# A decoder layer on one core: order of weight splits and gate sums where the norm phase meets the up-projection

## The chip, the core and the metric

The kernel runs on one core of a Trainium2 chip. Five engines work side by side, each with its own queue in fixed order: PE multiplies matrices (its weight loads show as PEld), DVE, ACT and POOL do elementwise work, SP issues loads. They wait for each other by semaphores. The metric is the time of one execution on the device in microseconds (us), lower is better.

## What is computed

One layer: an RMS norm and a projection into three branches (a recurrent one, stick-breaking attention, attention to memory tokens), a gated merge, and a feed-forward part with a causal convolution. The change lies in the feed-forward part:

```python
def conv_ffn(x, g, w_up, conv_w, conv_b, w_down):
    h = rms_norm(x, g) @ w_up            # 1024 x 1024 by 1024 x 5632
    t = h.shape[1]
    hp = jnp.pad(h, ((0, 0), (CONV_W - 1, 0), (0, 0)))
    acc = conv_b + hp[:, 0:t] * conv_w[0]
    for i in range(1, CONV_W):
        acc = acc + hp[:, i:i + t] * conv_w[i]
    gate, val = jnp.split(acc, 2, axis=-1)
    return (jax.nn.silu(gate) * val) @ w_down
```

## The kernel before

Every fp32 product is made of three matmuls: each operand is split into a rounded high part (made by ACT, a copy into fp32r) and the rest (POOL or DVE, a subtraction), and high x high, high x low and low x high are added up in PSUM.

The up-projection (`up_phase`) works through 22 pairs of 128-row blocks of the weight, gate pairs (even n) and value pairs (odd n) in turn. A pair takes seven products instead of eight (Strassen's way in Winograd's form), each of 4 x 3 = 12 matmuls of 128x512. Product (n, i) below is step i of pair n; step 4 is written 40 (the matmuls) and 41 (what follows them). Per pair the weights are two loaded tiles w1 and w2 (named `wr` for odd, `rw` for even n), from which come sums and differences:

- `prep1(n)` splits w1: high and low part `wh`, `wl`, for products 1 and 2;
- `prep2(n)` makes two sums on POOL (L1484, L1485, tile `it`) and splits them (`l`), for products 5 and 6;
- `prep3(n)` makes w1 - w2 in place (L1497) and s4 (L1498, tile `s`), and splits the first (`wh`, `wl`, products 7 and 4) and s4 (`l`, 512 wide, product 3).

All splits go through `hl`: its activation is L1462, its subtraction on POOL L1465. `keep` holds the activation at its place in the written order, `queue` the subtraction; without them a scheduler places the instruction.

What PE makes is taken up by DVE: L1585 adds product 6 and product 1's copy `p` into `u`, L1592 and L1593 make the second block's `u` from product 7, `p` and 5's bank, L1602 takes product 4 off, L1609 adds product 3's bank. PSUM banks are used again at once: product 7 accumulates on the bank of 6, so it waits for L1585; product 3 on the bank of 5, so it waits for L1593. Then `conv_half` makes the convolution: an activation (L1529), two steps on DVE (L1530, L1531), and for a gate pair a sigmoid (L1534) and a product (L1535), for a value pair a product (L1540) into `gall`. `act_sums` makes four sums of these results behind each value pair, on DVE (L1548), and stores seven tiles to `actd` from ACT's queue. The first two sums (`late` false) stood in step 3 of the pair, the other two in step 6 of the next, behind L1585.

The stretch in question is the seam: the norm phase's last operands, pair 0 and pairs 1 and 2 are written out by hand. On PE the order there is (0,7), (0,4), (0,3), (1,6), (1,5), (1,4), (1,7), (2,1), (1,3), (2,5), (2,6), (2,2), (2,7), (2,4), (2,3), (3,1). In the code `prep3(1)` stood behind step (0,3), and `prep1(2)` behind step (1,5).

Of the kernel before, what the change touches and what calls it, by code (L numbers as in the profile page):

```python
# [49 lines left out]
class Trunk:  # L50
# [1386 lines left out]
    def up_phase(self, raws, t2, operand, split_hi, split_lo, sums, norm, spread):  # L1437
# [11 lines left out]
        pairs = [(o + 2 * f, f, o > 0) for f in range(NF // 2) for o in (0, NF)]  # L1449
        W, st = {}, {}  # L1450
# [9 lines left out]
        def hl(src, pool, tags, n=1024, keep=False, queue=False):  # L1460
            hi, lo = (pool.tile([128, n], F32R, name=self.nm(t), tag=t, bufs=16 if t == "l4" else 2) for t in tags)
            ins = nc.scalar.activation(hi, src, AF.Copy)  # L1462
            if keep:
                self.pinned(ins)
            ins = nc.gpsimd.tensor_tensor(lo, src, hi.bitcast(F32), ALU.subtract)  # L1465
            if queue:
                self.tc.keep_in_program_order(ins)
            return hi, lo
# [1 line left out]
        L, R = slice(0, 512), slice(512, 1024)  # L1470

        def prep1(n):
            w = self.early[4 * n] if n < 2 else hl(W[n][0], self.pool_wt, ("wh", "wl"), queue=n == 2)
            st[n, 1], st[n, 2] = [[x[:, c] for x in w] for c in (L, R)]

        def prep2(n):
# [12 lines left out]
        def prep3(n):  # L1489
            if n == 0:  # L1490
                w2, s4 = self.early[2], self.early[3][:, R]
            else:
                w1, w2 = W.pop(n)
                s = st.pop((n, "s"))
                s4 = self.pool_r.tile([128, 512], F32, name=self.nm("s4"), tag="s4", bufs=1)
                fix = self.tc.keep_in_program_order if n == 1 else lambda ins: ins
                fix(nc.gpsimd.tensor_tensor(w2[:, L], w1[:, L], w2[:, L], ALU.subtract))  # L1497
                fix(nc.gpsimd.tensor_tensor(s4, w1[:, R], s[:, R], ALU.subtract))  # L1498
            w = hl(w2, self.pool_wt, ("wh", "wl"), queue=n == 1)
            st[n, 7], st[n, 4] = [[x[:, c] for x in w] for c in (L, R)]  # L1500
            if n:
                st[n, 3] = hl(s4, self.pool_l, ("l4", "l4"), 512)

# [9 lines left out]
        def bank():  # L1513
            return self.ps("mm")
# [31 lines left out]
        def act_sums(f, late):  # L1546
            a11, a21, a12, a22 = (g_all[:, j] for j in range(4))
            tt = lambda o, x, y, op: self.pinned(nc.vector.tensor_tensor(o, x, y, op))  # L1548
            if not late:
                tt(sa[:, 0], a21, a22, ALU.add)  # L1550
                tt(sa[:, 1], sa[:, 0], a11, ALU.subtract)
                for j, src in ((0, a11), (1, a12), (3, a22)):
                    nc.scalar.dma_start(self.actd[f, j], src)
            else:
                tt(sa[:, 2], a11, a21, ALU.subtract)
                tt(sa[:, 3], a12, sa[:, 1], ALU.subtract)
                nc.scalar.dma_start(self.actd[f, 2], sa[:, 3])
                nc.scalar.dma_start(self.actd[f, 4:7].rearrange("i p t -> p i t"), sa[:, 0:3])
# [7 lines left out]
        def step(n, i):  # L1566
            if i == 1:
                A = st[n, "A"] = bank()
                product(n, 1, A, True, True)
                if n:  # L1570
                    evacuate(n)
            elif i == 2:
                A = st.pop((n, "A"))
                product(n, 2, A, False, True)
                u = st[n, "u1"] = u_tile(n < 2)
                nc.scalar.activation(u[:, L2], A, AF.Copy)
            elif i == 5:
                C = st[n, "C"] = bank()
                product(n, 5, C, True, True)
            elif i == 6:  # L1580
                Bk = st[n, "B"] = bank()
                product(n, 6, Bk, True, True)
                if (n, "u1") not in st:
                    st[n, "u1"] = u_tile()
                self.pinned(nc.vector.tensor_tensor(st[n, "u1"][:, R2], Bk, st[n, "p1"], ALU.add))  # L1585
                if n and pairs[n - 1][2]:
                    act_sums(pairs[n - 1][1], True)
            elif i == 7:
                Bk = st.pop((n, "B"))
                product(n, 7, Bk, False, True)  # L1590
                v = st[n, "u2"] = u_tile()
                nc.vector.tensor_tensor(v[:, L2], Bk, st.pop((n, "p1")), ALU.add)  # L1592
                nc.vector.tensor_tensor(v[:, R2], st[n, "C"], v[:, L2], ALU.add)  # L1593
            elif i == 40:
                Dk = st[n, "D"] = bank()
                product(n, 4, Dk, True, True)
            elif i in (4, 41):
                if i == 4:
                    step(n, 40)
                Dk = st.pop((n, "D"))  # L1600
                v = st[n, "u2"]
                nc.vector.tensor_tensor(v[:, L2], v[:, L2], Dk, ALU.subtract)  # L1602
                if n + 1 < len(pairs):
                    conv(n, 1, st.pop((n, "u2")))
            elif i == 3:
                C = st.pop((n, "C"))
                product(n, 3, C, False, True)
                u = st.pop((n, "u1"))
                nc.vector.tensor_tensor(u[:, R2], C, u[:, R2], ALU.add)  # L1609
                if n + 1 == len(pairs):  # L1610
                    conv(n, 1, st.pop((n, "u2")))
                st[n, "gates"] = conv(n, 0, u)
                if pairs[n][2]:
                    act_sums(pairs[n][1], False)
                    if n + 1 == len(pairs):
                        act_sums(pairs[n][1], True)

# [56 lines left out]
        nc.vector.tensor_tensor(v[:, R2], st[0, "C"], v[:, L2], ALU.add)  # L1674
        step(0, 40)
        step(0, 41)
        load(2)
        step(0, 3)
        prep3(1)
        for n in range(1, len(pairs)):  # L1680
            order = {1: (6, 5, 40, 7, 41, 3), 2: (5, 6, 2, 7, 4, 3)}.get(n, (1, 5, 6, 2, 7, 4, 3))
            nxt = n + 1
            more = nxt < len(pairs)
            for i in order:
                if i == 2:
                    u1_first(n)
                else:
                    step(n, i)
                if not more:
                    continue  # L1690
                if i == 5:
                    load(nxt + 1)
                if (n, i) == (1, 5):
                    for close in st.pop((0, "gates")):
                        close()
                elif (n, i) == (1, 41):
                    step(nxt, 1)
                if i == (6 if n > 1 else 7):
                    prep2(nxt)
                if i == (2 if n > 1 else 5):  # L1700
                    prep1(nxt)
                if i == 3:
                    prep3(nxt)
# [332 lines left out]
```

## Time and profile before

| | |
|---|---|
| time, median of 3 runs | 1805.65 us (1805.49 to 1806.79) |
| the profiled execution | 1808.55 us |
| its span, first to last instruction | 1806.8 us |
| granted clock of PE, mean | 0.996 |
| DMA, mean | 145 GB/s |

PE's waits beside those of the seam are short. In the list of who waited for whom, a row has the waiting engine and line, what it waited for, and the total, the count and the longest in us:

```profile
PE mm L115 <- POOL wl L81: 2.3, 1, 2.3
PE g L115 <- ACT at L920: 2.2, 3, 1.0
PE mm L115 <- DVE at L1286: 1.6, 3, 0.6
```

How the other rows are read: a row of the timeline has the start and the length in us, the engine, the line, the operation, out<-in and the count of instructions merged into it; in brackets the idle time before it and what ended that. A row of a window has its bounds and length, the busy time of PE, PEld, DVE, ACT and POOL (with counts), the granted clock, the DMA share and GB/s. Names lose their numbers there, so `wh<-wr` is the high part of any odd pair's tile.

### The profile page before, as it was taken

To read this page: it belongs to the slowest core of one execution; us is meant where nothing else is said; L and a number is where in the kernel's file an instruction comes from. 1 tells how busy PE (TensorE), PEld (TensorE's weight loads), DVE (VectorE), ACT (ScalarE), POOL (GpSimd) and SP (SyncE) were. 2 spreads that over 40 slices of the span, in tenths; PEclk is the share of its full clock that TensorE was granted. 3 is DMA by queue.
4 is the path that set the end of the run, shared out by engine and by line. 5 is a ranking of instruction groups with operands and counts; after the bars stand their busy time and mean duration, and the time that the engine had idled before them with its cause. 6 is when DMAs were issued, how large, how long until landed. Compare 5 with 4: busy or idle time off the path is not lost.

```text
span 1806.8 us, 27325 instructions
## 1 busy us (share of the span) xinstructions
PE 1783.4 (99%) x10479; PEld 1446.0 (80%) x10479; DVE 1182.9 (65%) x1626; ACT 864.3 (48%) x1556; POOL 791.7 (44%) x448
## 2 busy tenths in 40 slices
PE   9999999999999999999999999989999999999999
PEld 7777778888888888777777878867888888888887
DVE  5667775898987534244443872577776777795596
ACT  6444344566566535534444334543544444454343
POOL 3223353322231462122333542486767767545454
PEclk9999999999999999999999999999999999999999
DMA  5255664211112352577654553222332323486476
GB/s 208 59 163 176 196 208 157 73 42 45 53 56 88 115 129 79 192 239 277 206 187 176 186 198 106 105 87 88 123 100 88 116 101 111 134 304 226 146 237 206
DMA packets 122772, 261.29 MB, mean 145 GB/s; under 512 B 28681, under 2 KB 43657, under 8 KB 122514
## 3 DMA queue, kind: packets, MB, share of 16 engines
q1 hardware_dynamic: 85026, 193.83, 32.7%
q10 hardware_dynamic: 33840, 53.10, 8.0%
q0 software_dynamic: 3776, 12.62, 2.3%
q8 instruction: 82, 1.34, 0.3%
q14 instruction: 48, 0.39, 0.1%
HBM read 178.99 MB, written 80.48 MB: 144 GB/s over the span
## 4 chain that ended last, share of the span: by engine, by line
PE 69%; DVE 7%; ACT 3%; issue 2%; POOL 2%; DMA 1%; SPq 0%; DVEq 0%; POOLq 0%; ACTq 0%
PE mm L115 57%; PE g L115 10%; PE g L105 2%; DVE at L926 1%; DVE it L545 1%; DMA wr<-in_w_out_dram 1%; DVE mg L1294 1%; POOL wl L81 1%; DVE inst L547 1%; DMA A<-yd 0%; ACT at L1143 0%; DVE w L821 0%; DVE at L1286 0%; DVE g L1530 0%; DVE at L1287 0%
## 5 line engine op out<-in xcount | busy, mean ns | idle before, releaser
L81 POOL TENSOR_TENSOR wl<-wr,wh 128x1024 fp32r<-128x1024 f32 (+2 forms) x78 | 195.9, 2512 | 501.5 <-ACT wh L80 492.0
L115 PE MATMUL mm<-xhi,wh 128*128 128x512 f32 x784 | 260.1, 413 | 0.5 <-DVE w L322 0.4
L115 PE MATMUL mm<-xlo,wh 128*128 128x512 f32 x784 | 243.5, 392 | 0.0
L115 PE MATMUL mm<-xhi,wl 128*128 128x512 f32 x784 | 242.5, 391 | 0.0
L115 PEld LDWEIGHTS mm<-xlo,wh 128*128 128x128 f32 x784 | 147.1, 188 | 33.2 <-DVE xlo L199 0.3
L115 PEld LDWEIGHTS mm<-xhi,wl 128*128 128x128 f32 x784 | 147.0, 188 | 33.0 <-POOL wl L81 0.7
L115 PEld LDWEIGHTS mm<-xhi,wh 128*128 128x128 f32 x784 | 136.7, 190 | 29.2 <-issue 6.1
L80 ACT ACTIVATE wh<-wr 128x1024 fp32r<-128x1024 f32 (+2 forms) x78 | 81.8, 1048 | 146.4 <-PE mm L115 93.3
L115 PE MATMUL mm<-dw,da 128*128 128x512 f32 x528 | 121.0, 390 | 0.0
L115 PE MATMUL mm<-BT,wh 128*128 128x512 f32 x352 | 111.8, 399 | 6.7 <-DVE u L1585 5.8
L115 PE MATMUL mm<-BT,l 128*128 128x512 f32 x504 | 117.6, 389 | 0.0
L115 PEld LDWEIGHTS mm<-dw,da 128*128 128x128 f32 x528 | 98.9, 188 | 21.5 <-DVE da L1746 1.0
L1747 POOL TENSOR_TENSOR dw<-draw,dw 128x512 fp32r<-128x512 f32 x55 | 81.9, 1497 | 77.3 <-ACT dw L1745 75.9
L926 DVE TENSOR_TENSOR_SCAN at<-at,nrt 128x128 f32<-128x128 f32 (+3 forms) x64 | 94.2, 1479 | 25.5 <-ACT at L920 25.3
L115 PEld LDWEIGHTS mm<-BT,l 128*128 128x128 f32 x504 | 94.6, 188 | 19.7
L115 PE MATMUL mm<-B,wh 128*128 128x512 f32 x352 | 108.6, 390 | 0.0
L1746 DVE TENSOR_TENSOR da<-draw,da 128x512 fp32r<-128x512 f32 x77 | 65.9, 862 | 53.2 <-ACT da L1744 52.9
L1465 POOL TENSOR_TENSOR l<-it,l 128x1024 fp32r<-128x1024 f32 x21 | 51.2, 2436 | 92.9 <-ACT l L1462 92.8
L115 PE MATMUL g<-dw,da 128*128 128x512 f32 x396 | 90.2, 389 | 0.0
L821 DVE TENSOR_TENSOR w<-w,nrt 128x1024 f32<-128x1024 f32 x24 | 49.9, 2078 | 58.1 <-ACT w L820 47.1
L115 PEld LDWEIGHTS g<-dw,da 128*128 128x128 f32 x396 | 74.3, 188 | 15.4
L1744 ACT ACTIVATE da<-draw 128x512 fp32r<-128x512 f32 x77 | 48.1, 627 | 80.4 <-PE mm L115 32.3
(335 smaller groups left out, 3990.9 us busy)
## 6 DMA issues: line engine op xcount, KB each, us to landing
wr<-in_w_in_dram SPq DMA_DIRECT2D x48, 512.0 KB, 3.6
draw<-actd SPq DMA_DIRECT2D x77, 256.0 KB, 3.3
draw<-in_w_down_dram SPq DMA_DIRECT2D x55, 256.0 KB, 4.5
at<-scr SPq DMA_DIRECT2D x24, 512.0 KB, 5.8
wr<-in_w_up_dram SPq DMA_DIRECT2D x22, 512.0 KB, 3.5
actd<-gall ACTq DMA_DIRECT2D x44, 256.0 KB, 3.3
rw<-in_w_up_dram SPq DMA_DIRECT2D x20, 512.0 KB, 3.7
gsd<-w ACTq DMA_DIRECT2D x18, 512.0 KB, 2.8
```

Source lines behind the costliest of these rows:

```text
L80: self.nc.scalar.activation(hi, raw, AF.Copy)
L81: self.nc.gpsimd.tensor_tensor(lo, raw, hi.bitcast(F32), ALU.subtract)
L105: self.pinned(self.nc.tensor.transpose(out, in_, self.ident[:n, :n]))
L115: self.pinned(self.nc.tensor.matmul(*a, **k))
L545: self.pinned(nc.vector.tensor_tensor(tv, X[:, 0:s, s : s + 1].to_broadcast([128, s, n]), X[:, s : s + 1, s + 1 : 64].to_broadcast([128, s ...
L547: self.pinned(nc.vector.tensor_tensor(X[:, 0:s, s + 1 : 64], X[:, 0:s, s + 1 : 64], tv, ALU.add))
L821: nc.vector.tensor_tensor(g, g, self.nrb, ALU.mult)
L926: self.pinned(nc.vector.tensor_tensor_scan(sn[:, :W][:, ::-1], sn[:, :W][:, ::-1], self.nrt[:, 1152 - W :][:, ::-1], 1.0, ALU.mult, ALU.max))
L1465: ins = nc.gpsimd.tensor_tensor(lo, src, hi.bitcast(F32), ALU.subtract)
L1744: self.pinned(nc.scalar.activation(A[:, 0], a, AF.Copy))
L1746: self.pinned(nc.vector.tensor_tensor(A[:, 1], a, A[:, 0].bitcast(F32), ALU.subtract))
L1747: nc.gpsimd.tensor_tensor(Wt[:, 1], w, Wt[:, 0].bitcast(F32), ALU.subtract)
```

## The change

`prep3(1)` now makes its two differences and splits w1 - w2 ahead of step (0,3), and hands s4 back; s4's split and `prep1(2)` follow behind step (0,3). The activations of the three are held in the written order. The first two sums of the first value pair (n = 1) leave its step 3 and stand behind L1585 in step 6 of pair 2, ahead of the other two. Nothing is computed that wasn't before, and the same number of instructions runs.

```diff
         def prep1(n):
-            w = self.early[4 * n] if n < 2 else hl(W[n][0], self.pool_wt, ("wh", "wl"), queue=n == 2)
+            w = self.early[4 * n] if n < 2 else hl(W[n][0], self.pool_wt, ("wh", "wl"), keep=n == 2, queue=n == 2)
...
-            w = hl(w2, self.pool_wt, ("wh", "wl"), queue=n == 1)
+            w = hl(w2, self.pool_wt, ("wh", "wl"), keep=n == 1, queue=n == 1)
             st[n, 7], st[n, 4] = [[x[:, c] for x in w] for c in (L, R)]
+            if n == 1:
+                return s4
             if n:
                 st[n, 3] = hl(s4, self.pool_l, ("l4", "l4"), 512)
...
                 if n and pairs[n - 1][2]:
+                    if n == 2:
+                        act_sums(pairs[n - 1][1], False)
                     act_sums(pairs[n - 1][1], True)
...
                 if pairs[n][2]:
-                    act_sums(pairs[n][1], False)
+                    if n > 1:
+                        act_sums(pairs[n][1], False)
...
         step(0, 41)
+        s4 = prep3(1)
         load(2)
         step(0, 3)
-        prep3(1)
+        st[1, 3] = hl(s4, self.pool_l, ("l4", "l4"), 512, True, True)
+        prep1(2)
...
-                if i == (2 if n > 1 else 5):
+                if n > 1 and i == 2:
                     prep1(nxt)
```

In the built program PE and SP keep their rows in the same order. ACT's queue moves at the seam. In the rows, `it` is pair 1's sum, `wr` and `s` its w1 - w2 and s4, `rw` pair 2's first tile, `u` with the lower number pair 0's first block, and the lines of the changed kernel are two higher (L1529 is L1531, L1534 is L1536). Before:

```order
L1462 ACTIVATE l_1626_10719<-it_10716 128x1024
L1462 ACTIVATE wh_10812<-wr_10638 128x1024
L1462 ACTIVATE wh_10853<-rw_10781 128x1024
L1529 ACTIVATE g_10769<-u_10750,params 128x512
L1529 ACTIVATE g_10775<-u_10750,params 128x512
L1529 ACTIVATE g_10799<-u_10653,params 128x512
L1462 ACTIVATE l_1643_10816<-s_1640_10809 128x512
L1534 ACTIVATE sg_10768<-g_10769 128x512
L1534 ACTIVATE sg_10768<-g_10775 128x512
L1529 ACTIVATE g_10804<-u_10653,params 128x512
```

and the same place of ACT's queue in the changed kernel:

```order
L1462 ACTIVATE l_1626_10719<-it_10716 128x1024
L1531 ACTIVATE g_10769<-u_10750,params 128x512
L1531 ACTIVATE g_10775<-u_10750,params 128x512
L1531 ACTIVATE g_10806<-u_10653,params 128x512
L1536 ACTIVATE sg_10768<-g_10769 128x512
L1536 ACTIVATE sg_10768<-g_10775 128x512
L1462 ACTIVATE wh_10784<-wr_10638 128x1024
L1531 ACTIVATE g_10811<-u_10653,params 128x512
L1536 ACTIVATE sg_10805<-g_10806 128x512
L1536 ACTIVATE sg_10805<-g_10811 128x512
L1462 ACTIVATE l_1643_10816<-s_1635_10781 128x512
L1462 ACTIVATE wh_10820<-rw_10788 128x1024
```

The splits of `wr`, `s` and `rw` moved behind three activations of the convolution and two to four sigmoids. Behind these rows ACT has, before and now, the high part of pair 2's sum, and now straight behind it that of pair 2's second tile, ahead of pair 1's convolution.

DVE's queue moves where pair 1's convolution ends and pair 2's add (L1585, now L1587) stands. Before:

```order
L1540 TENSOR_TENSOR gall<-g_10937,gall 128x512
L1548 TENSOR_TENSOR gall<-gall 128x512 x2
L1521 MEMSET u_10988 128x2
L1585 TENSOR_TENSOR u_10988<-mm_10975,p_1659_10917 128x512
L1548 TENSOR_TENSOR gall<-gall 128x512 x2
L1521 MEMSET u_11031 128x2
L1592 TENSOR_TENSOR u_11031<-mm_10975,p_1659_10917 128x512
```

and the same place of DVE's queue in the changed kernel:

```order
L1542 TENSOR_TENSOR gall<-g_10937,gall 128x512
L1523 MEMSET u_10983 128x2
L1587 TENSOR_TENSOR u_10983<-mm_10970,p_1659_10917 128x512
L1550 TENSOR_TENSOR gall<-gall 128x512 x4
L1523 MEMSET u_11031 128x2
L1596 TENSOR_TENSOR u_11031<-mm_10970,p_1659_10917 128x512
L1597 TENSOR_TENSOR u_11031<-mm_10953,u_11031 128x512
```

Two of the four sums moved from ahead of the add to behind it.

POOL's queue keeps its order but for one row. In the changed kernel it runs from s4's low part to the next pair's:

```order
L1465 TENSOR_TENSOR l_1644_10817<-s_1635_10781,l_1643_10816 128x512
L1465 TENSOR_TENSOR wl_10821<-rw_10788,wh_10820 128x1024
L1484 TENSOR_TENSOR it_10886<-rw_10789 128x512
L1485 TENSOR_TENSOR it_10886<-it_10886,rw_10788 128x512
L1497 TENSOR_TENSOR rw_10789<-rw_10788,rw_10789 128x512
L1498 TENSOR_TENSOR s_1662_10942<-rw_10788,it_10886 128x512
L1465 TENSOR_TENSOR l_1655_10890<-it_10886,l_1654_10889 128x1024
L1465 TENSOR_TENSOR wl_10946<-rw_10789,wh_10945 128x1024
L1484 TENSOR_TENSOR it_10995<-wr_10852 128x512
L1485 TENSOR_TENSOR it_10995<-it_10995,wr_10851 128x512
L1497 TENSOR_TENSOR wr_10852<-wr_10851,wr_10852 128x512
L1465 TENSOR_TENSOR l_1666_10950<-s_1662_10942,l_1665_10949 128x512
```

The low part of pair 2's second tile (`wl<-rw`, the eighth row) moved ahead of the three rows for pair 3 that follow it here.

## The prediction

> **What bounds the kernel now.** I read the page's busy times first, then the waits of PE, then the rows of the engines in order of time around the longest of these waits.
>
> ```profile
> PE 1783.4 (99%) x10479; PEld 1446.0 (80%) x10479; DVE 1182.9 (65%) x1626; ACT 864.3 (48%) x1556; POOL 791.7 (44%) x448
> PE mm L115 <- DVE u L1585: 5.8, 2, 3.6
> ```
>
> PE is the bound: 99% busy, so only its idle time and its slow stretches can be won. The largest entry of PE's waits, 5.8 us in two waits, is for the add at L1585, and both lie at the seam. PE's rows there:
>
> ```profile
> 1193.05 0.62 PE L115 MATMUL mm<-BT,wh 128*128 128x512 f32 x2
> 1193.51 0.39 PE L115 MATMUL mm<-BT,wl 128*128 128x512 f32 x1
> ...
> 1195.55 0.39 PE L115 MATMUL mm<-BT,wl 128*128 128x512 f32 x1
> 1199.58 1.22 PE L115 MATMUL mm<-BT,wh 128*128 128x512 f32 x2 [3.64 <-DVE u L1585]
> ...
> 1204.86 0.80 PE L115 MATMUL mm<-B,wh 128*128 128x512 f32 x2
> ...
> 1210.50 5.60 PE L115 MATMUL mm<-BT,l 128*128 128x512 f32 x24
> 1215.94 0.62 PE L115 MATMUL mm<-B,wh 128*128 128x512 f32 x2
> ...
> 1218.43 0.39 PE L115 MATMUL mm<-B,wl 128*128 128x512 f32 x1
> 1220.93 0.73 PE L115 MATMUL mm<-BT,wh 128*128 128x512 f32 x2 [2.12 <-DVE u L1585]
> ...
> 1228.15 2.88 PE L115 MATMUL mm<-B,l 128*128 128x512 f32 x12
> ```
>
> Two products (24 matmuls) start at 1210.50 and the next at 1215.94: 2.72 us a product, 0.227 a matmul. (1,7) could have started at 1195.55 + 0.22 = 1195.77; it ended at 1204.86, so this place lost 9.09 - 2.72 = 6.37 us. (2,7) could have started at 1218.66; it and (2,4) ended at 1228.15: 9.49 - 5.44 = 4.05 us. Together **10.42 us**, though PE idled only 5.76. The rest is the clock:
>
> ```profile
> 1198.40:1205.20 6.80, 5.62 (x13) 4.46 (x14) 2.52 (x6) 2.51 (x4) 6.64 (x6) 0.50 0.26 72
> 1222.30:1225.70 3.40, 3.40 (x10) 2.62 (x9) 1.73 (x3) 0.00 (x0) 3.40 (x3) 0.50 0.80 308
> 451.00:456.00 5.00, 4.21 (x38) 3.44 (x39) 4.97 (x3) 3.82 (x8) 1.79 (x1) 1.00 0.34 105
> 451.79 0.51 PE L115 MATMUL g<-qk,qk 128*128 128x256 f32 x2 [1.03 <-ACT at L920]
> ```
>
> The granted clock (third number from the end of a window's row) is 0.50 behind both waits, and 1.00 around a wait of 1.03 us. After 3.64 us the product took 1204.86 - 1199.58 = 5.28, 2.56 too much; after 2.12 us two products took 7.22, 1.78 too much.
>
> **The first wait.** Why was the add late?
>
> ```profile
> 1184.41 0.69 DVE L1602 TENSOR_TENSOR u<-u,mm 128x512 f32<-128x512 f32 x1 [0.91 <-PE mm L115]
> 1191.62 1.46 DVE L1530 SCALAR_TENSOR_TENSOR g<-u,params,g 128x512 f32<-128x512 f32 x2 [6.52 <-ACT g L1529]
> ...
> 1197.52 1.41 DVE L1531 SCALAR_TENSOR_TENSOR g<-u,params,g 128x512 f32<-128x512 f32 x2
> 1198.84 0.68 DVE L1585 TENSOR_TENSOR u<-mm,p 128x512 f32<-128x512 f32 x1
> 1188.91 1.06 ACT L1462 ACTIVATE wh<-wr 128x1024 fp32r<-128x1024 f32 x1 [3.92 <-POOL wr L1497]
> 1189.87 1.04 ACT L1462 ACTIVATE wh<-rw 128x1024 fp32r<-128x1024 f32 x1
> 1190.82 2.17 ACT L1529 ACTIVATE g<-u,params 128x512 f32<-128x512 f32 x3
> ...
> 1193.77 1.26 ACT L1534 ACTIVATE sg<-g 128x512 f32<-128x512 f32 x2 [0.22 <-DVE g L1531]
> 1190.09 2.40 POOL L1465 TENSOR_TENSOR wl<-wr,wh 128x1024 fp32r<-128x1024 f32 x1
> ```
>
> DVE's convolution waits for ACT, whose first convolution step stood behind two splits, the first of which (of pair 1's last weight, in wr) waited for POOL until 1188.9. In the changed order the convolution steps and their first two sigmoids come ahead of it, and the other split (pair 2's first weight, in rw) further behind still. The input of the convolution, L1602, is done at 1185.10, so the activations start at 1185.14, 5.68 earlier. Everything in this stretch of DVE moves with them: first step 1191.62 to 1185.94, L1585 1198.84 to 1193.16, done at 1193.84. PE wants it at 1195.77, so there is 1.9 us to spare and **6.37 us are won**. What is late next is the moved split: by the same shift the second sigmoid ends at 1195.03 - 5.68 = 1189.35, the split runs to 1190.35, its low part on POOL (2.40) to 1192.8. PE's third matmul of (1,4) wants it at 1193.51: hidden behind (1,6) and (1,5), with 0.7 to spare. Without that cover each microsecond of lateness would be one of PE. The last convolution activation, now queued behind the split, starts at 1190.3 and ends at 1191.0, just ahead of DVE's turn for it (1191.2). SP's queue keeps its rows and their order, and the rw tile has been in place since before 1189.87, so no load is late.
>
> **POOL falls behind.** POOL's next work is the low part of s4, whose high part ACT now makes behind the second pair of sigmoids. DVE's last step, now at 1198.93 - 5.68 = 1193.25, lets the last sigmoid go (half of 1.26), and the split of 128x512 takes another 0.6: ready at 1194.45.
>
> ```profile
> 1193.63 1.30 POOL L1465 TENSOR_TENSOR l<-s,l 128x512 fp32r<-128x512 f32 x1 [1.14 <-ACT l L1462]
> 1194.89 2.38 POOL L1465 TENSOR_TENSOR wl<-rw,wh 128x1024 fp32r<-128x1024 f32 x1
> 1197.22 1.27 POOL L1484 TENSOR_TENSOR it<-rw 128x512 f32<-128x512 f32 x1
> 1198.56 1.27 POOL L1485 TENSOR_TENSOR it<-it,rw 128x512 f32<-128x512 f32 x1
> 1199.78 1.30 POOL L1497 TENSOR_TENSOR rw<-rw,rw 128x512 f32<-128x512 f32 x1
> ...
> 1202.27 2.39 POOL L1465 TENSOR_TENSOR l<-it,l 128x1024 fp32r<-128x1024 f32 x1
> ```
>
> So this chain runs 0.86 later than before (1194.49 for 1193.63), while PE runs earlier. wl ends at 1198.13; (2,1) wants it at 1195.77 + 2.72 + 0.45 (two matmuls) = 1198.94: hidden behind (1,7), 0.8 to spare. The low part of pair 2's sum ends at 1202.27 + 0.86 + 2.39 = 1205.52; the third matmul of (2,5) wants it at 1195.77 + 3 x 2.72 + 0.45 = 1204.38. A **new wait of about 1.15 us**, near the 1.03 that left the clock alone.
>
> **The second wait.** L1585 of pair 2 no longer stands behind two sums. But the convolution ahead of it starts late:
>
> ```profile
> 1208.10 1.46 DVE L1530 SCALAR_TENSOR_TENSOR g<-u,params,g 128x512 f32<-128x512 f32 x2 [0.85 <-ACT g L1529]
> ...
> 1216.79 3.48 DVE L1548 TENSOR_TENSOR gall<-gall 128x512 f32<-128x512 f32 x2
> ```
>
> Its own input is ready when (1,7) has ended (1198.5) and three adds of 0.7 have followed, at about 1200.8. But ACT, in order, first makes the high part of pair 2's second weight, which waits for POOL's L1497, now until 1199.78 + 0.86 + 1.30 = 1201.94. Queued behind it stand pair 1's four convolution activations, for which DVE waits, and PE behind DVE. The split takes 0.95 (1188.91 to 1189.87), and DVE follows 0.80 behind the activation (1190.82 to 1191.62): it starts at 1203.7 instead of 1208.10. From there to where the sums stood is 8.69, so L1585 runs from 1212.4 to 1213.1. PE, with its 1.15, wants (2,7) at 1195.77 + 6 x 2.72 + 1.15 = 1213.25. No wait: **4.05 us are won**, by a hair.
>
> **The four sums.** They now stand behind L1585 in one row, and ahead of L1592 and L1593, without which (2,3) can't start. What they cost depends on POOL:
>
> ```profile
> 1257.66 1.42 DVE L1548 TENSOR_TENSOR gall<-gall 128x512 f32<-128x512 f32 x2
> 1259.01 0.69 DVE L1585 TENSOR_TENSOR u<-mm,p 128x512 f32<-128x512 f32 x1
> 1259.61 4.27 DVE L1548 TENSOR_TENSOR gall<-gall 128x512 f32<-128x512 f32 x2
> 1259.24 2.40 POOL L1465 TENSOR_TENSOR l<-it,l 128x1024 fp32r<-128x1024 f32 x1 [5.29 <-ACT l L1462]
> 1261.71 1.62 POOL L1484 TENSOR_TENSOR it<-rw 128x512 f32<-128x512 f32 x1
> ```
>
> Two sums take 1.42 with POOL idle and 4.27 with POOL at work: the second pair ends at 1263.88, 0.55 behind the end of L1484 (1263.33). So four cost between 2.8 and 8.5 us. I take the upper side, since POOL, being behind, has no pause: l<-it to 1205.5, wl to 1207.9, then at the steps of the rows above (1.34, 1.22, and 1.26 for the others of this size) L1484, L1485, L1497, l<-s, and L1498 from 1212.9 to 1214.2; then l<-it to 1216.9, and L1484 and L1485 at their stretched 1.62 to 1218.55 and 1220.25. A sum ends 0.55 behind each of the last four: the sums last from 1213.1 to **1220.8**, 7.7 us. L1592 and L1593 add 1.4 (two of 0.69), so (2,3) starts at 1222.2. PE wants it at 1213.25 + 5.44 = 1218.7: a **new wait of 3.5 us**, close to the old 3.64. Behind it the clock drops; the bounds are 1.78 (the 2.12 wait) and 2.56 (the 3.64 wait), and I take 2.2. The 1.15 is in PE's 1218.7 already, so the two waits add up: 10.42 - 1.15 - 3.5 - 2.2 = **3.6 us won**. The DMAs of the sums leave from the same place of ACT's queue, and (3,1) finds its weights in time: POOL's L1497 (1.62) and wl (2.40) end at 1224.3, wanted at 1222.2 + 2.72 + 0.45 = 1225.4. From there on the steps repeat as before, earlier by what was won.
>
> The profiled execution took 1808.55 (span 1806.8 and 1.75 around it), so it would take 1804.95. The timed median is 1805.65, 2.9 lower. Part of that may be slow clock that the timed executions don't have, so I take 0.6, a third of the 1.78 at the smaller old wait, off the gain: 3.0.
>
> One rule of the Trainium skill speaks for another price of the clock ("TensorE: Matmul & The Clock Gate", the part on the HAM clock gate): the clock falls to half after an idle window of about 3.4 us, in a grid that runs on its own. By it a wait of 3.5 would rarely cover a whole window, and the sum would be 5.8 in place of 3.6. The trace disagrees on the length: 2.12 us were enough for the row at 0.50.
>
> **The rivals.**
> - Sums free of POOL: if POOL pauses there, four sums take 2.8, no wait at (2,3), and only 1.15 is lost: 10.42 - 1.15 = 9.3, 1796.4. For it: 1.42 for two at 1257.66. Against it: POOL's row has no gap. Chance 0.10.
> - The clock stays up behind the new wait, as it did around the 1.03: then the 2.2 stays in hand, 5.8 - 0.6 = 5.2, 1800.4. For it: the window at 1.00. Against it: both waits over 2 us have their row at 0.50. Chance 0.10. That is also where the rule just named leads.
> - Waits in place of waits: ACT or POOL 1 us later than I have it uses up the 0.7 and 0.8, and PE waits at (1,4), (2,1) and longer at (2,3): gain 0 to 1, about 1805. Chance 0.17.
> - Slower: DVE gets in only at every second gap of POOL, a sum then lasting some 4.3 (2.59 + 1.70): 17.2 for 7.7 at the same place, so 9.5 more, less 3.0: 1812. It decides from sums of 7.7 + 3.0 = 10.7 us on. Against it: both sums in 4.27 got in at the first gap. Chance 0.05.
>
> **How the numbers follow.** My forecast has 0.58: 1805.65 - 3.0 = 1802.7. Its own range is 1800.8 to 1805.1: sums from 6.8 to 8.5 (a wait of 2.6 to 4.3), clock from 1.78 to 2.56, and from nothing to all of the 1.78 off for the timed runs give gains of 4.9 to 0.6. 0.2%, about what a measurement of this kernel can tell from no change, is 3.6 us: faster means under 1802.0. Of the forecast's 0.58 I put 0.20 there, with 0.10 and 0.10 of the first two rivals: 0.40. Within: 0.38 + 0.17 = 0.55. Slower 0.05. The range leaves out the first rival and the last: 1799.8 to 1806.0.
>
> **What would show it.** In the changed profile: no wait of PE for the add of L1585 (L1587 there), which starts near 1193.2 and 1212.4; PE waits about 1.15 for POOL's l at (2,5); about 3.5 for L1593's add (L1597) at (2,3); four sums in about 7.7 us; one stretch at 0.50 instead of two. I am wrong if the sums take under 5 us, or if wl of (1,4) or (2,1) shows among PE's waits.

## The result, and the profile after

| | before | changed |
|---|---|---|
| median of the timed runs | 1806.23 us (1803.08 to 1808.70, 13 runs) | 1801.92 us (1799.72 to 1804.97, 13 runs) |
| the profiled execution, its span | 1808.55, 1806.8 us | 1802.26, 1800.5 us |

The ratio is 0.9978 with a 95% interval of 0.9970 to 0.9986: 4.3 us faster. Two more sets of runs of the same kernel gave 0.9974 (0.9964 to 0.9983) and 0.9981 (0.9972 to 0.9990). The forecast was a gain of 3.0 and 1802.7 us. The mark of 0.2% between "faster" and "within" lies inside the interval; the prediction had put 0.40 and 0.55 on its two sides.

The busy times of the changed kernel's page, and two rows of its view of PE's waits (engine, line and what was waited for; us in total, times, longest):

```profile
PE 1778.4 (99%) x10479; PEld 1443.3 (80%) x10479; DVE 1183.7 (66%) x1626; ACT 864.3 (48%) x1556; POOL 791.5 (44%) x448
```

```profile
PE mm L115 <- DVE u L1597: 2.3, 1, 2.3
PE mm L115 <- POOL l L1465: 1.4, 1, 1.4
```

PE is as busy as before, 5.0 us less of it. The two waits for the add (L1585 before, L1587 now) are gone from the list. In their place stand one wait for POOL's low part, at (2,5), and one for the add at L1597, at (2,3): the two that were forecast as new. PE's rows at the seam, in order of time:

```profile
1188.18 5.60 PE L115 MATMUL mm<-BT,l 128*128 128x512 f32 x24
...
1206.53 5.28 PE L115 MATMUL mm<-BT,l 128*128 128x512 f32 x22 [1.41 <-POOL l L1465]
...
1222.23 3.01 PE L115 MATMUL mm<-B,l 128*128 128x512 f32 x12 [2.26 <-DVE u L1597]
1227.96 5.60 PE L115 MATMUL mm<-BT,l 128*128 128x512 f32 x24
```

The first row is (1,6) and (1,5), at 1188.18, where the execution of before has 1187.61; the prediction's times are therefore compared 0.57 later. From there to (2,3) it takes 34.05 us instead of 40.54. The last row is (3,5). In the execution of before it stands here:

```profile
1233.59 5.60 PE L115 MATMUL mm<-BT,l 128*128 128x512 f32 x24
```

From (1,6) to (3,5) lie 13 products. At the 2.72 us that the prediction read from the trace they need 35.36 us. What a kernel takes beyond that is called its **seam loss** below, waits and slow clock together: 10.62 us before (1233.59 - 1187.61 - 35.36) and 4.42 after (1227.96 - 1188.18 - 35.36).

DVE, ACT and POOL around the new waits:

```profile
1194.06 0.68 DVE L1587 TENSOR_TENSOR u<-mm,p 128x512 f32<-128x512 f32 x1
...
1204.69 1.46 DVE L1532 SCALAR_TENSOR_TENSOR g<-u,params,g 128x512 f32<-128x512 f32 x2 [3.29 <-ACT g L1531]
...
1213.27 0.68 DVE L1587 TENSOR_TENSOR u<-mm,p 128x512 f32<-128x512 f32 x1
...
1213.88 6.87 DVE L1550 TENSOR_TENSOR gall<-gall 128x512 f32<-128x512 f32 x4
...
1202.92 1.06 ACT L1462 ACTIVATE wh<-rw 128x1024 fp32r<-128x1024 f32 x1 [0.19 <-POOL rw L1497]
...
1204.11 2.37 POOL L1465 TENSOR_TENSOR l<-it,l 128x1024 fp32r<-128x1024 f32 x1
```

The reader is to see three things. The add runs at 1194.06 and 1213.27, early enough both times. ACT's split of pair 2's second weight starts at 1202.92, when POOL's L1497 has made its input, and only behind it does pair 1's convolution start. The four sums stand in one row of 6.87 us between the add and the next two adds, and PE waits behind these.

### The profile page after: what moved, and what is told of

Same layout as the page of the kernel before. It is cut to its first block, busy times and chain, and to the rows that moved or that the text cites. A ratio compares the mean times of both kernels' runs of the same rounds, so it can differ in the third digit from the quotient of the medians.

```text
span 1800.5 us, 27327 instructions
## 1 busy us (share of the span) xinstructions
PE 1778.4 (99%) x10479; PEld 1443.3 (80%) x10479; DVE 1183.7 (66%) x1626; ACT 864.3 (48%) x1556; POOL 791.5 (44%) x448
## 4 chain that ended last, share of the span: by engine, by line
PE 69%; DVE 6%; ACT 2%; issue 2%; POOL 2%; DMA 1%; SPq 0%; DVEq 0%; POOLq 0%; ACTq 0%
PE mm L115 57%; PE g L115 10%; PE g L105 3%; DMA wr<-in_w_out_dram 1%; DVE at L926 1%; DVE mg L1294 1%; DVE it L545 1%; DMA A<-yd 1%; DVE at L1287 0%; POOL wl L81 0%; POOL wl L1465 0%; DVE inst L547 0%; DVE gall L1550 0%; ACT at L1143 0%; DVE w L821 0%
```

## The experiments

The theory was that each of the two edits does its own part and that what is still lost hangs on POOL's row: the sums are stretched by it, (2,5) waits for it, and ACT's split waits for it with the convolution queued behind. The rivals were that one edit alone does all, that the sums' place is to blame, and that nothing can be won, since a load taken off one product is laid on the next. Each diff is against the changed kernel unless it says otherwise.

**The splits alone.** The sums stay where they were before.

```diff
-                    if n == 2:
-                        act_sums(pairs[n - 1][1], False)
                     act_sums(pairs[n - 1][1], True)
...
-                    if n > 1:
-                        act_sums(pairs[n][1], False)
+                    act_sums(pairs[n][1], False)
```

> The new order of the weight splits alone; the first two gate sums stay ahead of pair 2's add, as before. Theory A (one chain): from pair 1's convolution on, DVE's adds and four sums, stretched by POOL's work, are one chain that sets when (2,3) starts; where the sums stand only decides at which product PE waits. Then PE waits about 2.3 us for the add at (2,7), nearly nothing at (2,3), (2,3) starts within 0.7 us of the changed kernel's start (counted from (1,6)), and the time is within 1.5 us of the changed kernel's, so about 3 to 5 us under before. Theory B (two waits, each with its own edit): the splits win their 6.4 us of the first wait and no more, the second wait of 2.1 us with its slow clock stays as an addition, and the time is 2 to 4 us over the changed kernel's.

Measured: 1803.27 us, 0.9982 (0.9972 to 0.9993); seam loss 5.95. PE's rows:

```profile
1206.91 5.28 PE L115 MATMUL mm<-BT,l 128*128 128x512 f32 x22 [1.41 <-POOL l L1465]
...
1217.23 0.73 PE L115 MATMUL mm<-BT,wh 128*128 128x512 f32 x2 [2.32 <-DVE u L1587]
...
1224.43 2.88 PE L115 MATMUL mm<-B,l 128*128 128x512 f32 x12
```

The first wait goes with the splits alone, and the 1.41 at (2,5) comes with them. The second wait stays, since two sums still stand ahead of the add of pair 2. These are the waits of Theory A. (2,3) starts 35.87 us behind (1,6), 1.82 later than in the changed kernel and not within 0.7: in this execution a stretch of slow clock falls ahead of it, in which two products take 7.20 us instead of 5.44. The time is 2.5 us under before, less than the 3 to 5 of Theory A, and by the ratios to before 0.7 us over the changed kernel, less than the 2 to 4 of Theory B. The interval overlaps that of the changed kernel widely, so the times do not show what moving the sums adds to the splits.

**The sums alone.** The kernel before, with only the sums moved.

```diff
                 if n and pairs[n - 1][2]:
+                    if n == 2:
+                        act_sums(pairs[n - 1][1], False)
                     act_sums(pairs[n - 1][1], True)
...
-                    act_sums(pairs[n][1], False)
+                    if n > 1:
+                        act_sums(pairs[n][1], False)
```

> The gate sums moved behind pair 2's add alone; the splits stand as before. Both theories: the wait of 3.6 us at (1,7) stays. Theory A: the wait at (2,7) goes, but the four sums then run against POOL's work and PE waits about 1 to 2 us at (2,3); 0.5 to 2.5 us under before. Theory B: the second wait with its slow clock goes, 4 us under before.

Measured: 1805.67 us, 0.9994 (0.9984 to 1.0003); seam loss 9.10. PE's rows and DVE's sums:

```profile
1199.05 1.22 PE L115 MATMUL mm<-BT,wh 128*128 128x512 f32 x2 [3.65 <-DVE u L1585]
...
1225.98 3.00 PE L115 MATMUL mm<-B,l 128*128 128x512 f32 x12 [2.38 <-DVE u L1595]
...
1216.71 7.78 DVE L1548 TENSOR_TENSOR gall<-gall 128x512 f32<-128x512 f32 x4
```

The wait at (2,7) is gone, and one of 2.38 stands at (2,3): the move of the sums trades one wait for another. Alone its gain can't be told from none; Theory B's 4 us lie outside the interval. The rival that one edit does it all falls for the sums. For the splits it does not fall: alone they have most of the gain, and perhaps all.

**The sums two and two.** Two stay behind pair 2's add, two go behind the adds that (2,3) waits for.

```diff
-                    if n == 2:
-                        act_sums(pairs[n - 1][1], False)
-                    act_sums(pairs[n - 1][1], True)
+                    act_sums(pairs[n - 1][1], n > 2)
...
-                nc.vector.tensor_tensor(v[:, R2], st[n, "C"], v[:, L2], ALU.add)
+                self.pinned(nc.vector.tensor_tensor(v[:, R2], st[n, "C"], v[:, L2], ALU.add))
+                if n == 2:
+                    act_sums(pairs[1][1], True)
```

> The changed kernel, with the second two sums moved on behind L1593's add of pair 2 (two sums behind L1585, two behind L1593). Theory A: the two sums ahead of L1592 take about 3.5 us instead of 6.9 for four, the wait of 2.3 us at (2,3) in the changed kernel goes (under 0.5 is left), no new wait comes in its place, and the time is 1.5 to 3.5 us under the changed kernel's. Theory C (the wait at (2,3) is the late convolution's, not the sums'): the wait stays over 1.5 us and the time is within 0.7 us of the changed kernel's.

Measured: 1803.53 us, 0.9988 (0.9978 to 0.9998); seam loss 5.47. No gain over the changed kernel, a miss. PE's rows and POOL's:

```profile
1217.07 2.88 PE L115 MATMUL mm<-B,l 128*128 128x512 f32 x12
...
1222.91 0.50 PE L115 MATMUL mm<-B,wl 128*128 128x512 f32 x1 [2.51 <-POOL wl L1465]
...
1220.50 2.35 POOL L1465 TENSOR_TENSOR wl<-wr,wh 128x1024 fp32r<-128x1024 f32 x1
```

The two sums ahead of the adds took 2.38 us and (2,3) waits no more, so the sums had made that wait, and Theory C falls. But (3,1) waits 2.51 for the low part that POOL ends at 1222.85, and Theory A's "no new wait" was wrong. As long as PE had waited for the sums, this lateness of POOL had been hidden behind that wait.

**Pair 2's first weight split early.** Its split comes straight behind pair 1's last one, ahead of that of s4.

```diff
         load(2)
+        prep1(2)
         step(0, 3)
         st[1, 3] = hl(s4, self.pool_l, ("l4", "l4"), 512, True, True)
-        prep1(2)
```

> The changed kernel, with pair 2's first weight (wh and wl of rw) split straight behind pair 1's last, so that POOL has work in the 1.7 us in which it waits for s4's high part. Theory A: POOL's chain runs about 1.4 us earlier, so the wait of 1.4 us at (2,5) goes (under 0.3 is left); pair 1's convolution starts 1.4 us earlier too, the wait at (2,3) stays between 1.5 and 3.5 us, and the time is 1 to 2 us under the changed kernel's. Theory D (the wait at (2,5) comes from PE running earlier only, POOL's pause has no part in it): the wait stays over 1 us and the time is the same within 0.7 us.

Measured: 1801.03 us, 0.9978 (0.9965 to 0.9991); seam loss 4.38. PE's rows and the sums:

```profile
1205.28 5.88 PE L115 MATMUL mm<-BT,l 128*128 128x512 f32 x24
...
1221.55 4.58 PE L115 MATMUL mm<-B,l 128*128 128x512 f32 x12 [2.24 <-DVE u L1597]
...
1213.19 6.88 DVE L1550 TENSOR_TENSOR gall<-gall 128x512 f32<-128x512 f32 x4
```

The wait at (2,5) is gone: it was POOL's row, as the prediction had it, and Theory D falls. The sums and the wait behind them stay. The 1 to 2 us that were to be won over the changed kernel don't show: the ratio to before is the same 0.9978. In this execution the wait at (2,3) has the slow clock behind it (4.58 us for 12 matmuls), which the changed kernel's first had not.

**Both, and the changed kernel again.** The last two edits together, and beside them the changed kernel once more.

> Both earlier edits on top of the changed kernel: second two sums behind L1593, and pair 2's first weight split straight behind pair 1's last. Theory A (POOL's chain is the bound behind all of it): no wait at (2,5) and none at (2,3), but PE waits for POOL's low part wl of pair 3's first weight at (3,1), about 2.4 us (2.5 with the sums apart alone, less what is won and lost ahead of it); the time is within 1 us of the kernel with the early split alone. Theory B (each edit wins its own wait): no wait over 0.5 us is left at the seam, 3 to 4 us under the changed kernel.

> The changed kernel once more, beside the next three, as their measure and for the clock. The order of waits must be the same: 1.4 us at (2,5) for POOL, 2.0 to 2.5 us at (2,3) for L1597. Theory of the clock: whether such a wait is followed by a stretch at 0.50 differs from execution to execution with where it falls in a grid of 3.41 us; if instead the length alone decides, this wait leaves the clock at 1.00 again, as it did in the first profile of this kernel.

Measured: 1801.41 us for both edits, 0.9971 (0.9962 to 0.9980), seam loss 4.62; 1801.31 us for the changed kernel, 0.9974 (0.9964 to 0.9983), seam loss 5.86. In order, the row of both edits and that of the changed kernel's second execution:

```profile
1224.31 0.79 PE L115 MATMUL mm<-B,wl 128*128 128x512 f32 x1 [2.49 <-POOL wl L1465]
```

```profile
1220.51 4.58 PE L115 MATMUL mm<-B,l 128*128 128x512 f32 x12 [2.27 <-DVE u L1597]
```

With no wait left in pair 2, the whole of POOL's lateness shows at (3,1), as Theory A had it, and the time is within 1 us of the early split alone (1801.03). And the changed kernel, with the same wait of 2.27 us, this time has a slow stretch behind it, which its first execution had not (below).

**POOL's row held in another order.** As both edits before, and for pairs 3 and 4 POOL's queue is held in the written order, so that pair 3's low part stands ahead of pair 4's sums.

```diff
-            w = ... hl(W[n][0], self.pool_wt, ("wh", "wl"), keep=n == 2, queue=n == 2)
+            w = ... hl(W[n][0], self.pool_wt, ("wh", "wl"), keep=n == 2, queue=n in (2, 3))
...
-                fix = self.tc.keep_in_program_order if n == 2 else lambda ins: ins
+                fix = self.tc.keep_in_program_order if n in (2, 4) else lambda ins: ins
...
-                fix = self.tc.keep_in_program_order if n == 1 else lambda ins: ins
+                fix = self.tc.keep_in_program_order if n in (1, 4) else lambda ins: ins
```

> The kernel before this one, with POOL's queue held in the written order for pairs 3 and 4, so that the low part of pair 3's first weight comes ahead of L1484, L1485 and L1497 of pair 4, which PE wants a pair later. Theory A: these three take 4.6 us of POOL, so wl comes some 4 us earlier, no wait over 0.5 us is left from (1,6) to (3,3), and the time is 2.5 to 5 us under the changed kernel's. If POOL's load as such were too much for this stretch, the wait would come back within pairs 3 or 4, for their l or wl, with 1.5 us or more.

Measured: 1801.70 us, 0.9971 (0.9960 to 0.9982). No gain over the changed kernel, a miss. There is no wait at all from (1,6) to (3,5), so the seam loss by the definition above is 0; (3,7) then waits, and ACT and DVE show for what:

```profile
1234.62 0.73 PE L115 MATMUL mm<-BT,wh 128*128 128x512 f32 x2 [2.21 <-DVE u L1523]
...
1231.68 1.06 ACT L1462 ACTIVATE l<-it 128x1024 fp32r<-128x1024 f32 x1 [3.24 <-POOL it L1485]
...
1233.26 0.69 DVE L1537 TENSOR_TENSOR gall<-g,sg 128x512 f32<-128x512 f32 x1 [3.43 <-ACT sg L1536]
1233.88 0.69 DVE L1587 TENSOR_TENSOR u<-mm,p 128x512 f32<-128x512 f32 x1
```

L1523 sets two columns of the same tile; the late instruction is L1587. (3,7) and (3,4) have taken 9.54 us when (3,3) starts at 1241.79, 4.10 more than two products need. ACT stands 3.24 us in front of a split whose input POOL has not made, and the sigmoid queued behind that split is what DVE waits for. Up to here the rival that the load is laid on the next product had it right for the longer wait: it went from (2,7) to (2,3) to (3,1) to (3,7). But this row also names the way in which it is handed on: a split in ACT's queue, ahead of work that DVE needs.

**The convolution ahead of the split.** The same pattern stands in the changed kernel at ACT's 1202.92. Here pair 2's second weight is held behind pair 1's convolution.

```diff
-            w = hl(w2, self.pool_wt, ("wh", "wl"), keep=n == 1, queue=n == 1)
+            w = hl(w2, self.pool_wt, ("wh", "wl"), keep=n in (1, 2), queue=n == 1)
```

> The changed kernel, with the high part of pair 2's second weight held behind pair 1's convolution on ACT. It tests the step that ACT's wait for L1497 holds up the convolution. If so, DVE's first step of that convolution starts about 1.2 us earlier (counted from (1,6)), and so does L1587; the scheduler then has the low part of this weight on POOL four rows later, so PE waits 0.5 to 1.5 us for it at (2,7), and under 0.8 at (2,3) instead of 2.3; 0.3 to 1.5 us under the changed kernel. If not, the first step starts within 0.4 us of where it did and the wait at (2,3) stays at 2 us or more.

Measured: 1800.22 us, 0.9972 (0.9962 to 0.9983), and seam loss 3.54. DVE's and PE's rows:

```profile
1200.42 1.46 DVE L1532 SCALAR_TENSOR_TENSOR g<-u,params,g 128x512 f32<-128x512 f32 x2 [1.70 <-ACT g L1531]
...
1209.61 7.24 DVE L1550 TENSOR_TENSOR gall<-gall 128x512 f32<-128x512 f32 x4
...
1185.49 5.60 PE L115 MATMUL mm<-BT,l 128*128 128x512 f32 x24
...
1203.52 5.29 PE L115 MATMUL mm<-BT,l 128*128 128x512 f32 x22 [1.09 <-POOL l L1465]
...
1212.95 0.50 PE L115 MATMUL mm<-BT,wl 128*128 128x512 f32 x1 [0.97 <-POOL wl L1465]
```

DVE's convolution starts 14.93 us behind (1,6), in the changed kernel 16.51: 1.58 earlier, and no wait at (2,3) although the sums take 7.24. So ACT's split did hold up the convolution. What POOL is late with shows in smaller waits, 1.09 and 0.97. The median is 1.1 us under that of the changed kernel in the same runs, with intervals that overlap.

**That and the early split of pair 2's first weight**, and the former once more.

> The order with pair 1's convolution ahead of pair 2's split (as in e7_conv_first), and pair 2's first weight split straight behind pair 1's last one (as in e4_rw_split_early). Both leave the computation as it is. Theory A (POOL's row is what is late: it starts the low part of pair 2's sum 1.45 us earlier, as it did in e4, and everything behind it): PE's wait of 1.09 us for POOL's l at (2,5) is gone, the wait of 0.97 for POOL's wl at (2,7) is gone or under 0.3, nothing waits at (2,3); from the start of (1,6) to the start of (2,3) 32.2 to 32.7 us, where e7's execution has 32.75 and the changed kernel's 34.05; no stretch at half clock at the seam; time 1798.5 to 1800.0 where e7 runs at 1800.2. Theory B (the load is kept: POOL or DVE gets it back at the next place): the waits come back at (3,1) or in the first products of pair 3, 1.0 us or more of them, and the time is that of e7 within 0.7 us.

> The kernel of e7_conv_first once more, beside e8 on one chip. Its waits are set by the order, so they come again: about 1.1 us at (2,5), 1.0 at (2,7), 0.3 at (3,1), none at (2,3), and no stretch at half clock at the seam; time 1799.5 to 1801.5.

Measured: 1798.73 us (1797.69 to 1799.84, 5 runs), 0.9958 (0.9946 to 0.9971), seam loss 2.46; the former alone 1800.73 us, 0.9971 (0.9960 to 0.9983), seam loss 4.12, with waits of 1.42 at (2,5) and 0.54 at (3,1) where 1.1 and 0.3 were expected. PE's rows with both, and POOL's ahead of (2,7):

```profile
1204.04 5.94 PE L115 MATMUL mm<-BT,l 128*128 128x512 f32 x24
...
1214.08 0.50 PE L115 MATMUL mm<-BT,wl 128*128 128x512 f32 x1 [0.93 <-POOL wl L1465]
...
1219.37 3.02 PE L115 MATMUL mm<-B,l 128*128 128x512 f32 x12
...
1223.12 0.50 PE L115 MATMUL mm<-B,wl 128*128 128x512 f32 x1 [0.27 <-POOL wl L1465]
...
1208.56 1.30 POOL L1465 TENSOR_TENSOR l<-s,l 128x512 fp32r<-128x512 f32 x1
1209.94 1.30 POOL L1498 TENSOR_TENSOR s<-wr,it 128x512 f32<-128x512 f32 x1
1211.19 2.84 POOL L1465 TENSOR_TENSOR wl<-rw,wh 128x1024 fp32r<-128x1024 f32 x1
```

The wait at (2,5) is gone, as expected, and nothing of its size comes back behind it. The wait of 0.93 at (2,7) was expected to go and stays: POOL makes that low part (wl<-rw, 1211.19) behind two other instructions of its queue. So the load is not simply kept: where the order of a queue makes the wait, changing the order takes it away.

**The last kernel again, beside the changed one on one chip.**

> The kernel of e8_conv_first_rw_early once more, beside the changed kernel on one chip. If its gain over the changed kernel is real (2.3 us less waiting at the seam: 0.93 and 0.27 us are left of 1.41 and 2.26, and no wait is long enough for the half clock), it lies 1.5 to 4 us under it: 1797.5 to 1800. If the 2.0 us by which it lay under e9 were chance, it lies within 1 us of the changed kernel. Its waits come again: about 0.9 at (2,7), 0.3 at (3,1), no stretch at half clock at the seam.

> The changed kernel a third time: 1.41 at (2,5), 2.26 at (2,3), with or without half clock behind the second, as the wait falls in the gate's windows; time 1801 to 1802.5.

Measured: 1799.19 us (1796.76 to 1801.01, 6 runs), 0.9965 (0.9952 to 0.9978), seam loss 1.91; the changed kernel 1801.71 us (1799.01 to 1803.20, 11 runs), 0.9981 (0.9972 to 0.9990), seam loss 5.52. Here the changed kernel waited 1.05 at (2,5), not the 1.41 of its first two executions, and its convolution started 16.15 us behind (1,6), so such figures move by some 0.4 us between executions of one kernel. In two sets of runs the version with the convolution ahead of the split and the early first weight has the lowest median, here 2.5 us under the changed kernel. The two intervals still overlap (0.9972 to 0.9978), so its size is not settled.

All versions with their seam loss, worked out as above from PE's rows, and the median:

| version | seam loss, us | of this at half clock, us | median, us | before in the same runs |
|---|---|---|---|---|
| before | 10.62 | 6.8 and 3.4 | 1806.23 | |
| sums alone | 9.10 | 6.8 | 1805.67 | 1805.80 |
| splits alone | 5.95 | 3.4 | 1803.27 | 1805.80 |
| changed, three executions | 4.42, 5.86, 5.52 | 0, 3.4, 3.4 | 1801.92, 1801.31, 1801.71 | 1806.23, 1806.25, 1805.79 |
| sums two and two | 5.47 | 3.4, in part behind (3,5) | 1803.53 | 1805.80 |
| first weight early | 4.38 | 3.4 | 1801.03 | 1805.80 |
| both of these | 4.62 | 3.4 | 1801.41 | 1806.25 |
| and POOL's row in another order | 0, then 4.10 at (3,7) and (3,4) | 3.4 | 1801.70 | 1806.25 |
| convolution first, twice | 3.54, 4.12 | 0, 0 | 1800.22, 1800.73 | 1806.25, 1806.20 |
| and first weight early, twice | 2.46, 1.91 | 0, 0 | 1798.73, 1799.19 | 1806.20, 1805.79 |

The third column is how long the clock stood at 0.50 at the seam; half of that is lost while PE works. The losses come from one execution each and the medians from many, so single rows differ by a microsecond or two; the order is nearly the same. With 1.7 taken off for a stretch of 3.4, the splits alone lose 4.2 and the changed kernel 4.4, 4.2 and 3.8: in the traces too, the sums' move adds nothing clear to the splits.

## Why the prediction was right, step by step

**The first wait: right.** The add was forecast at 1193.16 + 0.57 = 1193.73 and ran at 1194.06. PE did not wait at (1,7), and the half clock behind the old wait went with it. Neither (1,4) nor (2,1) waited, though only 0.7 and 0.8 us of cover had been counted. The splits alone show the same at (1,7), and with the sums alone the wait of 3.65 stays, so it is the splits that do it.

**POOL behind: right.** Forecast a wait of 1.15 at (2,5), measured 1.41. POOL's low part started at 1204.11 and ended at 1206.48, forecast 1205.52 + 0.57 = 1206.09. A later execution had 1.05, so the forecast lies within what one kernel shows. With the first weight early it was gone.

**The convolution held by ACT's split: right.** DVE was forecast at 1203.7 + 0.57 = 1204.3 and started at 1204.69, behind an idle time of 3.29 for ACT. Putting the split behind the convolution moved it forward, by 0.9 to 1.6 us in the executions of both. In the changed kernel the add of pair 2 started at 1213.27, forecast 1213.0, and (2,7) did not wait.

**The four sums: right place and cause, sized too long.** Forecast 7.7 us, measured 6.87, against 2.8 by the rival in which POOL leaves them alone; that rival fell in every kernel with four sums in a row (6.87 to 7.78). The last sum ended 0.55 behind an instruction of POOL, as forecast, but behind L1484 (1220.20) and not L1485: the shortest of the four sums took 0.68, so one got in ahead of L1498, which the forecast had already running, and there was one gap of POOL less to wait for. The wait at (2,3) came out at 2.26 for the forecast 3.5. The sums and the two adds behind them let (2,3) start 0.54 us earlier than forecast (34.05 us behind (1,6), forecast 34.59). The other 0.70 is PE's own: by its wait it wanted (2,3) at 1219.97, which is 31.79 behind (1,6), where the forecast had 31.09: 0.26 of it from the longer wait at (2,5), the rest from small gaps.

One rule of the Trainium skill bears on the cause ("SBUF — State Buffer", section "SBUF: two separate sides"): an instruction of VectorE with two inputs in SBUF and one of GpSimd that reads SBUF shut each other out for the whole instruction (VectorE is DVE here, GpSimd is POOL). The trace agrees: two sums took 1.42 us with POOL idle and four took 6.87 beside POOL, while the adds at L1596 and L1597, which take one input from a product in PSUM (mm), kept their 0.68 and 0.69 beside POOL's L1485 in the changed kernel:

```profile
1220.68 0.68 DVE L1596 TENSOR_TENSOR u<-mm,p 128x512 f32<-128x512 f32 x1
...
1221.39 0.69 DVE L1597 TENSOR_TENSOR u<-mm,u 128x512 f32<-128x512 f32 x1
...
1218.58 1.62 POOL L1484 TENSOR_TENSOR it<-rw 128x512 f32<-128x512 f32 x1
1220.28 1.60 POOL L1485 TENSOR_TENSOR it<-it,rw 128x512 f32<-128x512 f32 x1
```

**The clock: this is the step that was mis-sized.** The sum held 2.2 us for a slow stretch behind the wait at (2,3), between 1.78 and 2.56. The mean granted clock (third number from the end) behind that wait, in the changed kernel's first, second and third execution:

```profile
1222.30:1225.70 3.40, 3.40 (x15) 2.60 (x16) 2.55 (x4) 2.79 (x4) 3.40 (x3) 1.00 0.14 45
```

```profile
1220.60:1224.00 3.40, 3.40 (x9) 2.64 (x10) 2.55 (x4) 2.19 (x3) 3.40 (x3) 0.51 0.10 36
```

```profile
1219.40:1222.80 3.40, 3.40 (x11) 2.75 (x12) 2.55 (x4) 2.21 (x4) 3.40 (x3) 0.70 0.14 46
```

The stretch is there in two executions of three. (2,3) and (3,1) together take 7.16 us in the second (1227.67 - 1220.51) and 5.73 in the first (1227.96 - 1222.23). Two products need 5.44 by the prediction's count, so the term is 1.72 with the stretch and 0.29 without, not 2.2. The lower bound of 1.78 was right for a stretch of 3.4 us; the upper one of 2.56 came from the wait of 3.64, whose stretch lasted twice as long (1198.4 to 1205.2). The rival "the clock stays up" is right for the first execution and the forecast for the others. Whole times don't separate them: 1802.26 us without the stretch, 1802.01 and 1800.83 with it, since executions differ elsewhere too (the second reached (1,6) 1.73 us earlier than the first).

**The sum.** In the profiled executions the seam became 6.20 us shorter (10.62 to 4.42), for the forecast 3.6. The clock spent 1.91 less than forecast and the wait at (2,3) 1.24 less; the longer wait at (2,5) took 0.26 of it back, and small gaps the remaining 0.3. In the timed runs 4.3 us were won, for a forecast of 3.0. The median lies between the forecast's 1802.7 and the 1800.4 of the rival with the clock up. The profiled gain (6.29) is larger than the timed one because the profiled execution of before lay 2.32 us above its median and that of the changed kernel 0.34; the prediction had taken 0.6 off for this. How often the timed runs had the slow stretch has not been measured.

## What to carry to other kernels

When a wait is taken away, work out what is late next, engine by engine, before counting the gain: here waits of 3.64 and 2.12 us became waits of 1.41 and 2.26 us, and the next cures moved the longer one on to later products until the order of ACT's queue was changed. Look for a conversion that waits for a slow engine and stands in an in-order queue ahead of work that the bound engine needs; putting it behind that work, and giving the slow engine its input earlier, had together the lowest medians of all versions. Test each edit by itself: of the two here, the splits have most of the gain, and for the sums none could be shown. Waits of up to 1.42 us cost no more than themselves here, while most of those over 2 us cost about 1.7 us of slow clock besides, so two small waits can be cheaper than one long one.

## What the runs showed of the hardware that was not expected

**The same wait slows the clock in one execution and not in the next.** Waits of PE between 2.1 and 2.5 us had the slow stretch behind them in the execution of before (2.12), in the changed kernel's second and third (2.27, 2.26), with the splits alone (2.32), the sums two and two (2.51), the first weight early (2.24), both of these (2.49) and POOL's row in another order (2.21), but not in the changed kernel's first (2.26) nor with the sums alone:

```profile
1226.00:1229.40 3.40, 3.40 (x15) 2.81 (x16) 2.55 (x4) 2.75 (x5) 3.10 (x2) 1.00 0.60 177
```

That is the stretch behind the wait of 2.38. Waits of up to 1.42 us at the seam had none in any execution here.

The traces show what decides. In windows of 0.1 us the clock of the execution of before falls at 1198.41 and 1222.30 and comes back at 1205.23 and 1225.71. From one change to the next these are 2, 5 and 1 steps of 3.413 us; an earlier slow stretch, 624.97 to 628.38, ends 167 such steps ahead of 1198.41. So the clock changes on a grid of its own, with the same step in every execution that had two changes, but laid differently over the kernel each time. In the changed kernel's first execution the slow stretch of 624.24 to 627.65 puts a line of the grid 174 steps later at 1221.57, inside the wait at (2,3) (1219.97 to 1222.23). The first two rows are the two steps that share this wait, the third is the step that holds nearly all of it in the third execution:

```profile
1218.16:1221.57 3.41, 1.81 (x8) 1.15 (x7) 3.38 (x5) 0.34 (x1) 3.25 (x3) 1.00 0.48 186
1221.57:1224.98 3.41, 2.75 (x12) 2.30 (x13) 2.45 (x4) 2.79 (x4) 3.41 (x3) 1.00 0.37 131
```

```profile
1217.37:1220.78 3.41, 1.42 (x6) 1.24 (x7) 2.50 (x5) 1.80 (x3) 3.38 (x3) 1.00 0.77 290
```

PE stood still for 1.60 us and 0.66 us of the first two (3.41 less the busy time), and the clock stayed; it stood still for 1.99 of the third, and the clock fell at its end. In the eleven executions whose grid can be laid by a slow stretch (read from 20 to 1780 us), a step at full clock with up to 1.62 us idle was never followed by a slow one and a step with 1.88 or more always; of those between, one with 1.66 was, and others with 1.66, 1.80 and 1.81 were not. The wait of 2.38 with the sums alone was cut into 1.21 and 1.17. So here it is about half a step of idle time that counts, and where the grid cuts the wait. A step that is slow already needs less: behind 1.17 and 1.55 us idle in one, a second slow step followed the waits of 3.64 and 3.65.

The rule of the Trainium skill that the prediction named ("TensorE: Matmul & The Clock Gate", Part 1), an idle window of about 3.4 us on a grid of its own, has the grid and its step as the traces show them. On the idle time the measurement decides: 1.99 us of a window were enough.

**POOL pays for the sums too.** Its subtraction of 128x512 at L1498 took 1.66 us beside the four sums, for 1.30 where DVE ran no sums:

```profile
1214.04 1.66 POOL L1498 TENSOR_TENSOR s<-wr,it 128x512 f32<-128x512 f32 x1
```

```profile
1199.83 1.30 POOL L1498 TENSOR_TENSOR s<-rw,it 128x512 f32<-128x512 f32 x1
```

The first row is of the changed kernel, the second of the one with the convolution first. In the forecast of the sums L1498 had been counted at the shorter time.
